# Gated DeltaNet's scan on one Trainium2 core: decayed keys, or a decay factor on the product's rows

## The chip, the cores and the metric

The kernel runs on one core of a Trainium2 chip. The metric is the device time of one execution in microseconds. The kernel is one layer of a hybrid sequence model with 512 latent tokens, 256 context tokens and 1024 channels, all in float32. Most large products split each operand into two parts, so that one product is three passes on TensorE; the small products inside the scans are plain float32.

The engines are TensorE (PE, and PEld for its weight loads), VectorE (DVE), ScalarE (ACT), GpSimd (POOL) and SyncE (SP), which issues all DMA transfers. Each engine works through its own queue in order.

## The reference, cut to what matters

The layer has three token mixers side by side (HGRN2, gated DeltaNet, S5), each projected and gated, then an output projection and a channel sub-layer. The change touches the gated DeltaNet alone. It has four heads with keys and values of 128 channels, runs in both directions, and the scan of the latent tokens starts from the final state of the context's. Per chunk the reference does this:

```python
def step(s, inp):
    qc, kc, vc, bc, gc = inp
    cum = jnp.cumsum(gc, axis=-1)                      # summed log decays in the chunk
    ...
    kb = kc * bc[..., None]
    m = jnp.where(strict, -jnp.einsum('bhtd,bhsd->bhts', kb, kc) * dmask, 0.0)
    rhs = jnp.concatenate([vc * bc[..., None], kb * jnp.exp(cum)[..., None]], axis=-1)
    sol = lax.linalg.triangular_solve(eye - m, rhs, left_side=True, lower=True, unit_diagonal=True)
    u, w = sol[..., :dv], sol[..., dv:]
    v_new = u - jnp.einsum('bhtd,bhdv->bhtv', w, s)
    ...
    s = (s * jnp.exp(last)[..., None]
         + jnp.einsum('bhsd,bhsv->bhdv', kc * jnp.exp(last - cum)[..., None], v_new))
```

The kernel solves with the inverse X of the unit triangular matrix: `v_new = X (b (v - exp(cum) (k S)))`, where `exp(cum)` is one number per token (a row of the product `k S`), b is beta over the key's squared norm, and v is rescaled to fit. The factor of a token may be put on the key before the product with S, or on the row of the product after it.

## The kernel before, in words

A chunk is 128 tokens: chunks 0 and 1 are the context's, 2 to 5 the latent's. Class `GD` handles a pair of heads; there are two pairs, so the scan runs twice. Both directions and both heads of the pair are worked on together, so an array of a step is 128 x (2 directions, 2 heads, 128), that is 128x512.

`run` first makes decays, keys in token layout and the inverses X of three batches of two chunks (`decays`, `tokens`, `batch`, `invert`), then goes through six steps, i = -2 to 3: two of the context, four of the latent. The state S is there from i = -1 on, so five steps of a pair use it. A step is:

- L930: product pk of the keys with the state S, four units (direction, head), on PE, into PSUM
- L932: r = v - pk, on VectorE
- L939: product py of X with r, on PE
- L944: u = py times b, on VectorE
- L950, L954, L956 (L958 where there is no state yet): the next state, S times the chunk's decay plus a product of ke and u

`ahead` (L903) prepares one step ahead what doesn't need the state. For the five steps with a state it loads the summed log decays of the step's chunks from the DRAM array `gdrow`, broadcast onto all 128 partitions (`rows`, L779; 128x512 float32, 256 KB), takes their Exp in place (L910) and multiplies with the transposed keys (L911); the result R is the first operand of L930. For all steps but the last it makes the decayed keys ke in token layout (L914).

`out` loads rows of the same kind, for two chunks at once (512 KB), for the queries: Exp at L1002, products with the queries at L1006 and the output's products at L1017 and L1018. It is called twice per pair.

Everything is traced in the order of the program, and the Tile framework's scheduler then orders each engine's queue by readiness in its own model of time, so an instruction can stand ahead of one that comes earlier in the program. The scans are woven together with pieces of other work by `weave`: while a scan runs, projections (three passes L246, L247, L248) keep PE at work. Their weights come through `Stream`: a load of 512 KB, a copy to the high part on ScalarE (L225) and a subtraction for the low part on VectorE (L226). All `dma` calls (L63) go to SyncE's queue. Arrays come from pools by tag: "s2" has 12 buffers of 128x512, "s4" 8 of 128x1024.

Of the kernel before, what the change touches and what calls it, by code (L numbers as in the profile page):

```python
# [18 lines left out]
# which pieces go to which engine: adaLN's tiles (vector engine), (latent or context, block) of the modulated tokens'  # L19
# low parts, groups of the scan's inputs (GpSimd) and of its outputs (vector engine); after which of adaLN's tiles a  # L20
# tile of tokens is loaded
# [7 lines left out]
# columns of w_in  # L29
# [3 lines left out]
def ap(t, off, dims):  # L33
    """An access pattern on a tile's (or slice's) partitions, with free dims [step, count]."""
    return bass.AP(tensor=t.tensor, offset=t.offset + off, ap=[list(t.ap[0])] + [list(d) for d in dims])


class K:
    """What the parts share: engines, pools, constants."""

    #: buffers of a tag
# [23 lines left out]
    @contextmanager  # L65
    def queued(self, *engines):
        """What the block gives these engines comes after what they were given before it."""
        with ExitStack() as st:
            traced = self.nc.cur_bb.bb.instructions
            for e in engines:  # L70
                st.enter_context(self.tc.issue_after(next(i for i in reversed(traced) if i.engine == e.engine)))
            yield


# ---------------------------------------------------------------- small arithmetic

class Names:
    """Names for the arrays of a tile [128, n, w]."""
# [14 lines left out]
def exp_precise(v, out, x, s):  # L93
    """exp(x) to float32's accuracy, 0 under its range: powers of two and a polynomial."""
# [15 lines left out]
def inv_two_pi():  # L110
    """1 / (2 pi) as four constants of 12 bits each."""
# [10 lines left out]
def sincos_precise(v, sn, cs, y, s):  # L122
    """sin and cos of y: its turns are reduced with exact products, then polynomials."""
# [41 lines left out]
    # quarter turns  # L165
# [3 lines left out]
    v.scalar_tensor_tensor(cq, w, 4.0, cq, op0=OP.is_equal, op1=OP.subtract)   # -cos  # L169
    v.tensor_scalar(sq, q, 1.0, None, op0=OP.is_equal)  # L170
    v.scalar_tensor_tensor(sq, q, -1.0, sq, op0=OP.is_equal, op1=OP.subtract)  # -sin
# [9 lines left out]
def rsqrt(v, out, x, t):  # L181
    """1 / sqrt(x), x > 0; three arrays of one shape."""
# [8 lines left out]
def cmul(v, outr, outi, ar, ai, br, bi, t):  # L191
    """Complex product; t is of the outputs' shape."""
# [8 lines left out]
# ---------------------------------------------------------------- products of split operands  # L201

class Stream:
    """Weights from DRAM, each split into two float32r parts that add up to it; a product of two
    split operands is three passes."""
# [13 lines left out]
    def split(self, w, engine=None):  # L219
        """Two parts of a tile of weights."""  # L220
# [8 lines left out]
    def load(self, w, col, nk, m=128, row=0):  # L229
        """The split block w[row:row + 128 nk, col:col + m], [128, nk, m]."""  # L230
# [4 lines left out]
def split_act(K, hi, lo, x, scale=None, engine=None):  # L235
    """hi + lo = scale * x."""
# [14 lines left out]
# ---------------------------------------------------------------- S5  # L251

class S5:
    """Chunks of 8 tokens. Partitions are (direction, state), or (token in chunk, channel of a group)."""
# [5 lines left out]
    def load(self, lam, b, c):  # L260
        """lam [128, 3 32]: its real and imaginary parts and the log of the step; b and c [128, 2 512]."""
# [10 lines left out]
    def params(self):  # L272
# [20 lines left out]
        # Bbar = ((a - 1) / lambda) B  # L293
# [21 lines left out]
        # powers by the token in the chunk: what it adds to the state after the chunk, times one  # L315
        # step more; and, the last token first, what that state gives at it
# [9 lines left out]
        # by blocks of 8 groups: [channel of a group, group, (token in chunk, chunk)], the context's chunks first  # L326
# [4 lines left out]
    def spread(self, e, x, p, g0, n, negate, o):  # L331
        """o [128, 2, n, (8 16)]: x [128, 2, G, 16] times p [128, 2, G, 8], complex; its imaginary part negated."""
# [55 lines left out]
    def taken(d, off, step, n):  # L388
        """An array [16, 8, ...] in DRAM as [(8 positions step apart, 16), 8, n]."""
        return bass.AP(tensor=d.tensor, offset=d.offset + off, ap=[[step, 8], [d.shape[-1], 128], [1, n]])  # L390

    def load_c(self, o):
        """C with its imaginary part negated, of both directions."""
# [6 lines left out]
    def spread_c(self, e, c, g0, n, o):  # L400
        """The parts of C's conjugate [128, 2, G, 16] times pout's: o [128, 2, n, (8 16)], its real part and its
        imaginary part's negative."""
# [9 lines left out]
    def taps(self):  # L412
        """The kernels of both directions over a chunk, in DRAM as [input channel, group, ...] with the lags in a row,
        the greatest first."""
# [5 lines left out]
        # Bbar of the two directions in columns 0..15 and 32..47  # L420
# [28 lines left out]
    def outputs(self):  # L449
        """-> self.dy: of the latent, as du, the last token of a chunk first."""  # L450
        K, G, n, m = self.K, self.G, 4, 8
        nc, v = K.nc, K.nc.vector
        # in the place of the context's states
# [44 lines left out]
# ---------------------------------------------------------------- HGRN2  # L498

class HG:  # L500
    """One head: q [128, 512] (twice the silu), F [128, 2 (bwd, fwd), 512], FC [128, 2, 256] of the
    context, V [128 tokens, 6 chunks, 128], the context's first. Chunks of 128; within one, both
    directions' decays to a common point between two blocks, for blocks of 1, 2, ... 64."""
# [35 lines left out]
    def levels(self):  # L539
        K, q, F, N = self.K, self.q, self.F, self.N  # L540
        nc, v = K.nc, K.nc.vector
        Q = self.Q = K.t("s4", [128, 2, N])       # q: suffix bwd, prefix fwd
        Y = self.Y = K.t("s4", [128, 2, N])       # k: suffix fwd, prefix bwd
# [28 lines left out]
        self.tot = tot                            # [128, (bwd, fwd), chunk]  # L572
# [23 lines left out]
    def out(self, norm_w, gate, dst):  # L596
        """Normed and gated, into dst [128 channels, 512] in DRAM. gate: twice its silu, [128, 512]."""
# [21 lines left out]
def norm_heads(K, out, po, nq):  # L619
    """RMSNorm over the last axis of po [128 tokens, 4, 128], which is twice the values, or has yet to  # L620
    be multiplied by nq [128, 4]; without the gain, and times 1/2, as the gate comes twice as large."""
# [17 lines left out]
# ---------------------------------------------------------------- gated DeltaNet  # L639

class GDScalars:
    """Per token: beta, the summed log decays, for all heads; columns (chunk, direction, head)."""

    def __init__(self, K, ba, a_log, dt_bias):
# [17 lines left out]
        # softplus(x) = max(x, 0) + 2 atanh(e / (2 + e)), e = exp(-|x|)  # L662
# [14 lines left out]
        # sums over the chunk up to each token, and from it  # L677
# [15 lines left out]
        # [(direction, pair of heads), chunk, (head, token)]  # L693
# [5 lines left out]
class GD:  # L699
    """Heads 2p and 2p + 1. Chunks of 128: 0, 1 are the context's, 2..5 the latent's. Keys, queries  # L700
    and values come as twice their silu. Directions 0 fwd, 1 bwd. A batch is two chunks, four units
    (chunk, head)."""

    def __init__(self, K, sc, p):
# [12 lines left out]
        self.sm = K.t("gsm", [128, 240], bufs=2)  # L717
# [15 lines left out]
    def two(x, y):  # L733
        """The arrays x and y of one tile, [128, ...] each, as [128, 2, ...]."""
# [3 lines left out]
    def tokens(self):  # L738
        """Keys into token layout, and the sums of squares of keys and queries; then what follows from them."""
# [27 lines left out]
        # beta / |k|^2, units (chunk, direction, head), and the same negated  # L767
# [4 lines left out]
        for d in range(2):  # L772
            v.tensor_tensor(self.bk[:, :, d], four(sc.beta)[:, :, d], n2, op=OP.mult)
        hv = hn.rearrange("p (c h) -> p c h", c=6)
# [186 lines left out]
    def run(self, norm_w, gate, dst):  # L961
# [6 lines left out]
        for d in range(2):  # L968
            K.nc.vector.tensor_copy(self.cum[:, :, d], cum[:, :, d])
# [676 lines left out]
```

## Time and profile before

| | |
|---|---|
| median of 3 runs | 1439.66 us (1438.58 to 1440.03) |
| span of the profiled execution | 1440.3 us |
| PE busy | 1283.4 us, 89% of the span |
| VectorE busy | 882.4 us, 61% |
| ScalarE busy | 505.7 us, 35% |
| GpSimd busy | 382.2 us, 27% |
| DMA | 163.94 MB, mean 114 GB/s |

The profiled execution is one run; its time is not listed apart from its span. Busy shares are means over stages with different limits, so the stretches in which PE stands still are read one by one. The scan of heads 0 and 1 lies at about 655 to 712 us, that of heads 2 and 3 at about 850 to 912 us. "PEclk" is the clock that TensorE was granted, as a share of full speed.

### The profile page before, as it was taken

How to read it: one execution, taken by the hardware profiler on the slowest of the kernel's cores; microseconds unless marked ns; L12 is line 12 of the kernel's file. 1: busy time of each engine (PE TensorE's matmuls, PEld its weight loads, DVE VectorE, ACT ScalarE, POOL GpSimd, SP SyncE). 2: the span in 40 equal slices, each digit the busy share in tenths (PEclk: the TensorE clock that was granted, in tenths of full speed). 3: DMA queues.
4: the chain of work that ended last, by engine and by line, in shares of the span. 5: the costliest groups of instructions: out<-in, count | busy, mean ns of one | idle time of the engine just before them, and what ended most of it. 6: DMA issues, size and time to landing. Idle time of an engine off the chain costs nothing. (4 is left out here: it accounts for less than half of the span.)

```text
span 1440.3 us, 18357 instructions
## 1 busy us (share of the span) xinstructions
PE 1283.4 (89%) x6829; PEld 1053.9 (73%) x6829; DVE 882.4 (61%) x1683; ACT 505.7 (35%) x887; POOL 382.2 (27%) x510
## 2 busy tenths in 40 slices
PE   7687999999899898898877979976999999999995
PEld 2376767888787786797655968854777888888884
DVE  7733387866669658895559756526777432544336
ACT  3427413432334455312244342313225422244222
POOL 0345699994006710000004550003104000000002
PEclk9899999999999899999989979989999999999998
DMA  7672342738647666824466684696406433333231
GB/s 296 110 153 45 47 62 40 112 51 65 105 72 118 75 159 136 100 31 84 115 107 222 211 173 91 149 193 221 139 27 184 127 94 96 91 100 103 91 100 60
DMA packets 184987, 163.94 MB, mean 114 GB/s; under 512 B 24960, under 2 KB 155200, under 8 KB 184896
## 3 DMA queue, kind: packets, MB, share of 16 engines
q1 hardware_dynamic: 184896, 162.76, 51.7%
q8 instruction: 54, 0.88, 0.3%
q14 instruction: 37, 0.30, 0.1%
HBM read 143.86 MB, written 18.87 MB: 113 GB/s over the span
## 5 line engine op out<-in xcount | busy, mean ns | idle before, releaser
L226 DVE TENSOR_TENSOR lo<-raw,hi 128x1024 fp32r<-128x1024 f32 (+1 forms) x161 | 190.5, 1184 | 264.3 <-ACT hi L225 264.0
L225 ACT ACTIVATE hi<-raw 128x1024 fp32r<-128x1024 f32 (+1 forms) x161 | 157.5, 979 | 392.0 <-PE pj L247 230.1
L246 PE MATMUL pj<-hh,hi 128*128 128x512 f32 (+1 forms) x520 | 216.9, 417 | 13.8 <-ACT hi L225 7.3
L247 PE MATMUL pj<-hl,hi 128*128 128x512 f32 (+1 forms) x520 | 214.8, 413 | 0.9 <-POOL hl L1153 0.8
L248 PE MATMUL pj<-hh,lo 128*128 128x512 f32 (+1 forms) x520 | 214.2, 412 | 0.9 <-DVE lo L226 0.9
L247 PE MATMUL pj<-hc,hi 128*128 128x512 f32 (+2 forms) x536 | 188.2, 351 | 1.7 <-DVE hc L239 0.8
L246 PE MATMUL pj<-h,hi 128*128 128x512 f32 (+1 forms) x304 | 117.1, 386 | 12.7 <-ACT hi L225 11.6
L246 PEld LDWEIGHTS pj<-hh,hi 128*128 128x128 f32 (+1 forms) x520 | 101.8, 196 | 33.8 <-ACT hi L225 8.3
L248 PE MATMUL pj<-h,lo 128*128 128x512 f32 (+1 forms) x304 | 116.8, 385 | 3.4 <-DVE lo L226 3.1
L247 PEld LDWEIGHTS pj<-hl,hi 128*128 128x128 f32 (+1 forms) x520 | 101.8, 196 | 21.3 <-POOL hl L1153 2.4
L248 PEld LDWEIGHTS pj<-hh,lo 128*128 128x128 f32 (+1 forms) x520 | 101.7, 196 | 21.2 <-DVE lo L226 1.6
L247 PEld LDWEIGHTS pj<-hc,hi 128*128 128x128 f32 (+1 forms) x536 | 102.3, 191 | 16.2 <-DVE hc L1153 1.2
L246 PE MATMUL pj<-hc,hi 128*128 128x256 f32 (+2 forms) x264 | 85.8, 325 | 17.9 <-ACT hc L238 10.1
L1589 POOL TENSOR_TENSOR xn<-x,row 128x512 f32<-128x512 f32 x8 | 10.4, 1303 | 313.0 <-DVE x L1493 307.0
L248 PE MATMUL pj<-hc,lo 128*128 128x256 f32 (+2 forms) x264 | 85.5, 324 | 2.9 <-DVE lo L226 2.9
L1296 POOL TENSOR_TENSOR s<-s,raw 128x1024 f32<-128x1024 f32 x21 | 53.4, 2548 | 121.1 <-ACT raw L1295 111.3
L246 PEld LDWEIGHTS pj<-h,hi 128*128 128x128 f32 x304 | 57.8, 191 | 26.9 <-ACT hi L225 15.4
L248 PEld LDWEIGHTS pj<-h,lo 128*128 128x128 f32 x304 | 58.0, 191 | 17.3 <-DVE lo L226 6.8
L246 PEld LDWEIGHTS pj<-hc,hi 128*128 128x128 f32 (+1 forms) x264 | 50.9, 193 | 21.8 <-ACT hc L238 10.3
L248 PEld LDWEIGHTS pj<-hc,lo 128*128 128x128 f32 (+1 forms) x264 | 50.9, 193 | 6.6 <-DVE lo L226 3.7
L239 POOL TENSOR_TENSOR act<-raw,act 128x1024 fp32r<-128x1024 f32 x8 | 19.2, 2396 | 133.3 <-PE pj L247 110.5
L383 POOL TENSOR_TENSOR sw<-sp,sv 128x64 f32<-128x64 f32 x94 | 52.1, 554 | 0.0
(533 smaller groups left out, 2771.5 us busy)
## 6 DMA issues: line engine op xcount, KB each, us to landing
raw<-in_w_in SPq DMA_DIRECT2D x72, 512.0 KB
raw<-in_w_ff SPq DMA_DIRECT2D x64, 512.0 KB
raw<-in_ada_w SPq DMA_DIRECT2D x40, 512.0 KB
s<-gdrow SPq DMA_DIRECT2D x18, 256.0 KB
dg<-fg SPq DMA_DIRECT2D x16, 256.0 KB
fg<-dg SPq DMA_DIRECT2D x16, 256.0 KB
mg<-fg SPq DMA_DIRECT2D x16, 256.0 KB
fg<-mg SPq DMA_DIRECT2D x16, 256.0 KB
```

The lines of the kernel that those rows point to most:

```text
L225: K.nc.scalar.activation(hi, w, AF.Copy)
L226: (engine or K.nc.vector).tensor_tensor(lo, w, hi.bitcast(FT), op=OP.subtract)
L239: (engine or K.nc.vector).tensor_tensor(lo, x, hi.bitcast(FT), op=OP.subtract)
L246: nc.tensor.matmul(out, wh, xh, start=start, stop=False)
L247: nc.tensor.matmul(out, wh, xl, start=False, stop=False)
L248: nc.tensor.matmul(out, wl, xh, start=False, stop=stop)
L383: e.tensor_tensor(t[:, 0], aa[:, 0], x, op=OP.mult)
L1296: nc.gpsimd.tensor_tensor(acc, acc, w, op=OP.add)
L1589: nc.gpsimd.tensor_tensor(t[:, s], x1[i][:, s], fw[:, s], op=OP.mult)
```

## The change

The five decayed-key arrays of a pair are no longer made. L930 takes the plain transposed keys, and the factor exp(cum) of a token is applied when the product leaves PSUM: four instructions with a factor per row (one for each direction and head) compute `pk * ec - v` in place of one subtraction `v - pk`. The result has the opposite sign, and L944 takes a negated b (`nbk`) in the steps that have a state. The factors `ec` (24 columns) are one Exp of the summed log decays per pair, `nbk` one negation per pair; the small array `gsm` grows from 240 to 244 columns. `rows` loses the form for a step; `out` and `decays` still use it. The rest of the diff takes out comments.

```diff
@@ GD.tokens
             v.tensor_tensor(self.bk[:, :, d], four(sc.beta)[:, :, d], n2, op=OP.mult)
+        v.tensor_scalar(at(220, 24), at(100, 24), -1.0, None, op0=OP.mult)
@@ GD.rows
-    def rows(self, tag, c, d=None):
+    def rows(self, tag, c):
-        R = K.t(tag, [128, 2, 4, 128] if d is None else [128, 2, 2, 128])
+        R = K.t(tag, [128, 2, 4, 128])
-        step = 256 * (c[1] - c[0])
-        if d is not None:
-            K.dma(R, at(0, [[3072 + step, 2], [1, 256]]))
-        elif step == 256:
+        if c[1] == c[0] + 1:
@@ GD.ahead
-    def ahead(self, i, ch, final):
+    def ahead(self, ch, final):
-        nc, v = K.nc, K.nc.vector
-        R = ke = None
-        if i > -2:
-            R = self.rows("s2", ch, 0)
-            nc.scalar.activation(R, R, AF.Exp)
-            v.tensor_tensor(R, R, self.two(self.kT(ch[0]), self.kT(ch[1])), op=OP.mult)
-        if not final:
-            ke = K.t("s2", [128, 2, 2, 128])
-            v.tensor_tensor(ke, self.two(self.kt(ch[0]), self.kt(ch[1])), self.wide(self.el, ch), op=OP.mult)
-        return R, ke
+        if final:
+            return None
+        ke = K.t("s2", [128, 2, 2, 128])
+        K.nc.vector.tensor_tensor(ke, self.two(self.kt(ch[0]), self.kt(ch[1])), self.wide(self.el, ch), op=OP.mult)
+        return ke
@@ GD.step
-                    nc.tensor.matmul(pk[:, d, h], R[:, d, h], S[:, d, h], start=True, stop=True)
+                    nc.tensor.matmul(pk[:, d, h], self.kT(ch[d])[:, h], S[:, d, h], start=True, stop=True)
             r = K.t("s2", [128, 2, 2, 128])
-            v.tensor_tensor(r, vt, pk, op=OP.subtract)
+            for d in range(2):
+                for h in range(2):
+                    v.scalar_tensor_tensor(r[:, d, h], pk[:, d, h], self.ec[:, ch[d], d, h:h + 1], vt[:, d, h],
+                                           op0=OP.mult, op1=OP.subtract)
-        v.tensor_tensor(u, py, self.wide(self.bk, ch), op=OP.mult)
+        v.tensor_tensor(u, py, self.wide(self.bk if S is None else self.nbk, ch), op=OP.mult)
@@ GD.run
-        self.cum, self.el, self.last = four(124), four(148), four(172)
+        self.cum, self.el, self.last, self.ec, self.nbk = (four(o) for o in (124, 148, 172, 196, 220))
+        K.nc.scalar.activation(self.sm[:, 196:220], self.sm[:, 124:148], AF.Exp)
-        nxt = self.ahead(-2, order[0], False)
+        nxt = self.ahead(order[0], False)
-            now, nxt = nxt, self.ahead(i + 1, order[i + 3], i == 2) if i < 3 else None
-            yield from self.step(i, order[i + 2], *now)
+            now, nxt = nxt, self.ahead(order[i + 3], i == 2) if i < 3 else None
+            yield from self.step(i, order[i + 2], now)
```

## Rows read from the trace of the kernel before

**Rows 1.** The page, part 1: busy us (share of the span) x instructions

```profile
PE 1283.4 (89%) x6829; PEld 1053.9 (73%) x6829; DVE 882.4 (61%) x1683; ACT 505.7 (35%) x887; POOL 382.2 (27%) x510
```

**Rows 2.** Busy time by stretch, heads 0 and 1; columns in the first line

```profile
core 0: us, PE busy (x) PEld busy (x) DVE busy (x) ACT busy (x) POOL busy (x), PEclk, DMA share, GB/s
...
659.90:665.70 5.80, 0.04 (x1) 0.00 (x0) 1.29 (x2) 1.26 (x2) 0.00 (x0) 0.75 0.20 46
665.70:670.20 4.50, 4.46 (x19) 4.08 (x20) 1.89 (x3) 0.00 (x0) 0.00 (x0) 0.57 0.20 48
...
686.40:692.90 6.50, 0.23 (x2) 0.02 (x1) 3.25 (x6) 3.63 (x5) 0.00 (x0) 0.78 0.12 42
692.90:697.10 4.20, 4.20 (x14) 3.72 (x15) 2.95 (x4) 0.00 (x0) 0.00 (x0) 0.52 0.22 62
```

**Rows 3.** Order of time, first hole: start, duration, engine, line, [idle <-releaser]

```profile
657.49 1.06 PE L939 MATMUL mm<-s,s 128*128 128x128 f32 x8
...
659.54 0.40 PE L247 MATMUL pj<-hl,hi 128*128 128x512 f32 x1
663.73 0.63 ACT L910 ACTIVATE s<-s 128x512 f32<-128x512 f32 x1 [9.69 <-DMA s<-gdrow]
664.39 0.69 DVE L911 TENSOR_TENSOR s<-s,s 128x512 f32<-128x512 f32 x1 [6.01 <-ACT s L910]
...
665.00 0.68 DVE L944 TENSOR_TENSOR s<-mm,gsm 128x512 f32<-128x512 f32 x1
...
665.74 2.08 PE L954 MATMUL mm<-s,s 128*128 128x128 f32 x8 [5.80 <-DVE s L944]
```

**Rows 4.** Order of time, second hole

```profile
688.57 0.63 ACT L910 ACTIVATE s<-s 128x512 f32<-128x512 f32 x1 [11.49 <-DMA s<-gdrow]
...
689.85 1.06 ACT L1002 ACTIVATE s<-s 128x1024 f32<-128x1024 f32 x1 [0.66 <-DMA s<-gdrow]
...
690.94 0.69 DVE L1006 TENSOR_TENSOR s<-s,hc 128x512 f32<-128x512 f32 x1 [0.42 <-ACT s L1002]
...
691.55 0.68 DVE L1185 SCALAR_TENSOR_TENSOR s<-pst,pj 128x512 f32<-128x512 f32 x1
692.15 0.68 DVE L932 TENSOR_TENSOR s<-hc,mm 128x512 f32<-128x512 f32 x1
...
692.88 2.08 PE L939 MATMUL mm<-s,s 128*128 128x128 f32 x8 [6.26 <-DVE s L932]
```

**Rows 5.** Third hole, heads 2 and 3: two stretches, VectorE and PE in order

```profile
863.90:866.90 3.00, 0.19 (x2) 0.06 (x1) 1.40 (x3) 2.06 (x3) 0.27 (x1) 1.00 0.62 122
866.90:871.00 4.10, 4.10 (x15) 3.49 (x16) 4.07 (x6) 0.63 (x1) 0.00 (x0) 0.58 0.36 116
...
865.50 0.69 DVE L911 TENSOR_TENSOR s<-s,sv 128x512 f32<-128x512 f32 x1 [3.16 <-ACT s L910]
...
866.85 1.44 PE L954 MATMUL mm<-s,s 128*128 128x128 f32 x8 [2.81 <-DVE s L944]
```

**Rows 6.** Durations: lines by ns min/median/max, and four of L849 in order

```profile
L910 ACT ACTIVATE s<-s x10: 616/629/632, 663.7 to 878.8; 128x512 f32<-128x512 f32 x10
...
L932 DVE TENSOR_TENSOR s<-sv,mm x5: 677/687/689, 861.0 to 906.0; 128x512 f32<-128x512 f32 x5
...
L592 DVE SCALAR_TENSOR_TENSOR hs<-hs,ht,mm x24: 336/346/349, 268.4 to 512.6; 128x128 f32<-128x128 f32 x24
...
571.51 1.10 DVE L849 TENSOR_SCALAR s<-upper,gu 128x128 f32<-128x128 f32 x4
```

**Rows 7.** SyncE's DMA issues in order of time, around the second hole

```profile
677.36 0.37 SPq L63 DMA_DIRECT2D raw<-in_w_in  x1
677.79 4.89 SPq L63 DMA_DIRECT2D s<-gdrow  x3
```

**Rows 8.** After the scans: ScalarE's longest wait (us, times, longest), one stretch

```profile
ACT h L238 <- DMA t<-nb: 21.4, 4, 14.0
...
940.00:950.00 10.00, 6.96 (x24) 5.05 (x23) 4.50 (x6) 3.33 (x5) 0.00 (x0) 0.83 0.96 174
```

More of the change, by code (lines that the diff above doesn't have):

```diff
@@ L716, in __init__ @@
         self.vtc, self.ktc = (b.rearrange("p (c h d) -> p c h d", c=2, h=2) for b in base[5:7])
-        self.sm = K.t("gsm", [128, 240], bufs=2)
+        self.sm = K.t("gsm", [128, 244], bufs=2)
         self.sk = self.sm[:, 0:12].rearrange("p (c h) -> p c h", c=6)
@@ L901, in wide, with step @@
         return self.two(x[:, ch[0], 0], x[:, ch[1], 1])[:, :, :, None].to_broadcast([128, 2, 2, 128])
-    def ahead(self, i, ch, final):
+    def ahead(self, ch, final):
         K = self.K
-        nc, v = K.nc, K.nc.vector
-        R = ke = None
-        if i > -2:
-            R = self.rows("s2", ch, 0)
-            nc.scalar.activation(R, R, AF.Exp)
-            v.tensor_tensor(R, R, self.two(self.kT(ch[0]), self.kT(ch[1])), op=OP.mult)
-        if not final:
-            ke = K.t("s2", [128, 2, 2, 128])
-            v.tensor_tensor(ke, self.two(self.kt(ch[0]), self.kt(ch[1])), self.wide(self.el, ch), op=OP.mult)
-        return R, ke
-    def step(self, i, ch, R, ke):
+        if final:
[3 more added lines that the diff above has]
+        return ke
+    def step(self, i, ch, ke):
         K = self.K
```

## The prediction

> **What bounds the kernel now.** The page comes first: TensorE (PE) is busy for 89% of the span and VectorE (DVE) for 61% [rows 1]. A kernel of this kind gains where PE stands still, so the next view is the busy time by stretch over the two scans that the change touches (heads 0 and 1 near 655 to 712 us, heads 2 and 3 near 850 to 912 us). Heads 0 and 1 have two holes: PE has 0.04 us of work in one stretch of 5.8 us and 0.23 us in one of 6.5 us, and after each it runs for 4.5 and 4.2 us with a granted clock of 0.57 and 0.52 [rows 2]. These are parts at about half speed (the 1.2 GHz level), so a hole costs more than its width.
>
> The third view is the order of time around each hole. In the first, PE's last products for the context step (L939) are over at 658.6 us. Their eviction (L944) needs nothing else, yet it starts at 665.00, because VectorE works in order and L911, the product of keys and decay, stands ahead of it. L911 waits for the Exp of L910, which waits 9.69 us for the broadcast load of the decay rows. PE's L954 waits for L944 all that time: 5.80 us idle [rows 3]. So a transfer for the *next* step holds up the *present* one.
>
> The second hole has the same head: L910 waits for its load until 688.57, then L911. But more stands there. L1002, the Exp of the rows for the output product, waited for a load of its own until 689.85; behind it on VectorE are L1006 and L1185, and only then L932, on which PE's L939 waits: 6.26 us [rows 4].
>
> The third, in the scan of heads 2 and 3, is a small one like the first: L911 at 865.50 behind its Exp, then L944, with 2.81 us of PE idle inside a 3.0 us stretch and 4.1 us at clock 0.58 behind it [rows 5]. Elsewhere in both scans PE is full: the projections woven in hide the steps.
>
> **The change part by part.** Gone in each pair of heads, for five steps: the 256 KB broadcast load of decay rows, its Exp (0.629 us) and the product with the keys, which has the form of L932 (128x512, 0.687 us) [rows 6]. The state product L930 keeps its shape; only its first operand is another array.
>
> *First hole.* Without L910 and L911, L944 follows L939 at once, near 658.6, and is over at 659.3. PE has woven-in work until 659.9, so L954 starts with no hole. Saved: 5.80 idle, and the slow part: 4.5 x (1 - 0.57) = 1.9 [rows 2, 3]. Sum 7.7 us. Next late is the eviction L958 behind L954, which already has products of a projection beside it.
>
> *Third hole.* The same, since L944 stood behind L911 alone: 2.81 + 4.1 x (1 - 0.58) = 1.7, sum 4.5 us [rows 5].
>
> *Second hole.* Whole, it is 6.26 + 4.2 x (1 - 0.52) = 2.0, that is 8.3 us [rows 2, 4]. It goes whole only if L932 no longer stands behind L1006. If VectorE's order stays, L1002 still waits for its 512 KB of rows. What was in flight was the weights' load of 512 KB, the 256 KB for step 2, these 512 KB and the 256 KB for step 3, all issued from 677.4 to 682.7 [rows 7], and landed by 689.85, some 12 us for 1536 KB. Without the two of 256 KB a third of the bytes is gone. The one issued ahead is worth 12 x 256/1536 = 2.0 us; the one behind overlaps only the end, taken at half, 1.0. The bounds are 0 and 4.0, I take 3.0, an estimate from these rows. Then L932's first quarter is also ready 0.34 us earlier than the whole was (below). The hole shrinks by 3.3 us to 2.9; the slow part behind it is then like that of the third hole, 1.7 instead of 2.0. Saved 3.6 with the order as it stands, 8.3 with L932 ahead. A planner builds the orders, and lighter queues on SyncE, ScalarE and VectorE move it somewhat; I take 5.0, nearer to the order that the trace shows.
>
> The loads behind others in one queue deserve a sentence of the Trainium skill. The page "DMA: Bandwidth & Descriptors", section "Queues, rings and completion order", says that descriptors on a ring are consumed in order; by that alone only the load issued ahead would delay L1002's, the hole would shrink by 2.3 and the sum would be 1.0 us smaller. No row here separates the two.
>
> *Added on VectorE.* One subtraction of 128x512 (0.687 us) becomes four multiply-subtracts of 128x128 from PSUM with a factor per row. The trace has that form: L592 takes 0.346 us. How closely four follow each other is seen at L849, four of 128x128 in 1.10 us, so the four end after about 0.346 + 3 x 0.25 = 1.1 us [rows 6]. VectorE's own work falls: ten steps at 1.1 - 2 x 0.69 give -2.7 us; it is not the bound there. On the path the last quarter of r is 0.42 us later and the first 0.34 earlier. PE's L939 takes its four units one after another and needs the last some 0.7 us after the first, and in the undisturbed steps its start is covered by projection products. So I take 0. The ends are ten steps at +0.42, +4.2 us, if PE meets the last quarter each time, and ten at -0.34, -3.4 us, if the first decides; both stay for the range.
>
> A rule of the Trainium skill speaks against this part: "VectorE: DVE Perf Modes", section "Rules for kernel authors", wants the number of VectorE instructions kept small, and its section on the errata gives each one a fixed cost. With the page's fitted (N + 151)/0.96 ns four of 128 cost 1.16 us and one of 512 0.69 us. The trace agrees within 0.1 us [rows 6], so by the page the sum would lose at most 4.7 us, if no step were hidden.
>
> *Small edits.* Two Exps of 24 columns (each at most L910's 0.629) and two negations (each at most L592's 0.346) come before the batches, off the scans: 0 taken, at most 2.0 us [rows 6]. The sign of r is undone in L944's factor: no instruction. Where a factor is read from a small array that VectorE or ScalarE wrote over a hundred microseconds earlier, nobody waits.
>
> *Queues and buffers.* Ten loads leave SyncE's queue. One issue there stood blocked for a buffer while the weights' load was queued behind it, but the weights' load waits for a buffer of its own in the same place, so no more is counted. Ten fewer buffers of the tag "s2" are used; keys are read until L930 of the last step, but queries in the same buffer are read later still by L1006, so nothing is held longer.
>
> *Does it reach the end?* All engines work in order, and loads are issued when PE's work frees buffers, so what a scan gains shifts what follows. The last branch begins with the scan's result read back from DRAM: ScalarE waits 21.4 us for it [rows 8]. There the transfers are 0.96 busy [rows 8], the one place where a shift may be lost in part; since these loads too are released by the stage before them, I take nothing off.
>
> Sum: 7.7 + 5.0 + 4.5 = 17.2 us. The profiled execution spans 1440.3 us; its time is not listed apart from the three runs (1438.58 to 1440.03 us), and the span is 0.6 us above their median. 1440.3 - 17.2 - 0.6 = 1422.5 us.
>
> **The rivals.** (a) *All three holes go.* The planner puts L932 ahead of L1006. For it: L1006 has no hurry. Against it: it stood ahead in the trace. 7.7 + 8.3 + 4.5 = 20.5, 1419 us, and to 1416 with the early first quarter.
>
> (b) *The wait for the output's rows takes the place of the one removed.* L1002 stays where it is, its load lands no sooner, and the quarters cost their +4.2 on the path. For it: that load was as late as L910's, 1.3 us apart [rows 4]. Against it: a third of the bytes is gone. 7.7 + 4.5 - 4.2 = 8.0, 1431.7 us.
>
> (c) *Slower.* With ten issues and ten Exps gone, the planner, which holds transfers to be quicker than the trace shows, places the Exps of the output rows (two in each pair, L1002) earlier, before their data are there. ScalarE's queue then stands at them, and behind it L225, the splitting of the weights, on which PE's projections wait, as well as VectorE's L1006 ahead of L932 and L944. Each such Exp that is waited for costs a hole like the first or second, about 8 us. From three new holes on (24 against 20.5 saved) the kernel is slower: with four, 1439.7 - 20.5 + 32 = 1451 us; with three and the quarters' 4.2, 1447. Against it: these loads need buffers that are free only when batches are done.
>
> (d) *It doesn't do what it says for the time.* The releaser is inferred; if PE at the three places really waited for weights, the holes stay and nothing but the quarters changes: 1438 to 1441 us. Against it: L944's own input was there 6.4 us before it started [rows 3].
>
> **How the numbers follow.** Forecast as above 0.45, its own range 1417 to 1428; (a) 0.20; (b) 0.20; (c) 0.08; (d) 0.07. The range is 1414 to 1437 us: from (a) with the quarters' gain and a little of order elsewhere, to (b) with a few us lost in the stage of the transfers; it leaves out (c), (d) and a little at the lower end. A difference of 0.2% (2.9 us) is about what a measurement of this kernel can tell from no change. Faster by more 0.84, within it 0.08, slower 0.08.
>
> **What would show it.** Right: no L910 or L911 lines; L944 starts less than 1 us after L939 in the context steps; no PE hole over 1 us in the first and third place, granted clock 1.00 through them; a hole of 0 to 3 us before L939 of the second latent step, ended by L932 behind L1006; four lines of about 0.35 us at the subtraction; the stages behind 720 us shifted whole. Wrong: PE waiting for L944 or L939 as long as before, with L1002 waiting over 3 us for its load, or new waits of L225 behind it.

## The result and the profile after

The changed kernel takes 1419.51 us (median of 4 runs, 1418.70 to 1422.16). The kernel before takes 1439.53 us beside it, the ratio is 0.9872 with a 95% interval of 0.9855 to 0.9888. That is 20.0 us less; 17.2 were forecast, and 1422.5 us lies 3.0 us above the result.

In after's profile every line of the scan stands 3 to 8 lines higher: L930 is now L922, L932 is L927 (four instructions), L939 is L935, L944 is L940, L954 is L950; L1002 and L1006 of `out` are L999 and L1003. The page's part 1 of after, busy us (share of the span) x instructions, against [rows 1]:

```profile
PE 1277.2 (90%) x6829; PEld 1048.5 (74%) x6829; DVE 879.2 (62%) x1705; ACT 501.2 (35%) x879; POOL 381.5 (27%) x510
```

PE has the same 6829 products and VectorE 22 instructions more. What changed is when PE works. Busy time by stretch in after, at the places of [rows 2] and [rows 5] (stretch, length, busy us of PE, PEld, DVE, ACT, POOL, granted clock, DMA share, GB/s):

```profile
640.00:660.00 20.00, 20.00 (x154) 18.79 (x153) 16.40 (x25) 6.12 (x10) 0.00 (x0) 1.00 0.47 72
660.00:680.00 20.00, 20.00 (x119) 16.63 (x117) 14.72 (x27) 4.04 (x5) 1.69 (x2) 1.00 0.25 48
680.00:700.00 20.00, 20.00 (x131) 17.17 (x129) 11.04 (x35) 3.52 (x11) 0.00 (x0) 1.00 0.34 53
...
840.00:860.00 20.00, 20.00 (x116) 17.18 (x116) 15.13 (x29) 4.89 (x6) 1.75 (x2) 0.96 0.41 85
860.00:880.00 20.00, 20.00 (x125) 17.41 (x124) 11.24 (x31) 3.32 (x11) 0.00 (x0) 1.00 0.59 91
```

The third number is PE's busy time: 20.00 of 20 us in all five stretches. The same view of before, second and third stretch:

```profile
660.00:680.00 20.00, 14.26 (x78) 12.41 (x79) 10.85 (x17) 3.32 (x5) 1.70 (x2) 0.83 0.17 34
680.00:700.00 20.00, 13.73 (x72) 11.43 (x71) 8.87 (x13) 3.63 (x5) 0.00 (x0) 0.83 0.36 85
```

All three holes are gone, the second too, and with them the slow parts. (The 0.96 comes from the first two microseconds of its stretch, at 0.59; they follow short waits of PE near 831 and 835 us, 0.9 us for L890 and 0.8 for L225, neither at the place of a hole. From 842 us on the clock is 1.00.)

The order of time in after around the places of the first and the second hole (start, duration, engine, line, [idle before it <-releaser]; SPq rows are DMA issues; in a long row, which joins several, a later one stood blocked):

```profile
653.57 0.37 SPq L63 DMA_DIRECT2D raw<-in_w_in  x1
653.99 0.78 SPq L63 DMA_DIRECT2D s<-gdrow  x1
673.76 0.37 SPq L63 DMA_DIRECT2D raw<-in_w_in  x1
...
658.61 1.06 PE L935 MATMUL mm<-s,s 128*128 128x128 f32 x8
...
659.71 0.69 DVE L940 TENSOR_TENSOR s<-mm,gsm 128x512 f32<-128x512 f32 x1 [0.21 <-PE mm L935]
...
660.45 1.16 PE L950 MATMUL mm<-s,s 128*128 128x128 f32 x8
...
671.01 1.05 ACT L999 ACTIVATE s<-s 128x1024 f32<-128x1024 f32 x1
...
674.94 1.29 DVE L1003 TENSOR_TENSOR s<-s,hc 128x512 f32<-128x512 f32 x2
...
679.75 1.12 DVE L927 SCALAR_TENSOR_TENSOR s<-mm,gsm,hc 128x128 f32<-128x128 f32 x4
```

First place: the eviction L940 now waits only 0.21 us for its own product, where L944 had stood for 6 us behind L911 [rows 3], and L950 follows without idle time. Second place: on VectorE the order is still the one forecast, L1003 stands ahead of L927. But L999 waits for nothing. The load of its rows was issued at 653.99, 17 us before, and ahead of the next weights' load, which got its buffer only at 673.76. In the kernel before it was issued at 678.41, behind a weights' load and a load of decay rows, the first of the three in the row [rows 7].

Where the rest of the time went is read from the waits of PE over both scans, 640 to 920 us (line waited for: us in total, times, longest), here of before, without the lines of [rows 3] to [rows 5], which come to 14.9 us:

```profile
PE pj L246 <- ACT hc L238: 10.1, 1, 10.1
PE mm L892 <- DVE s L893: 8.7, 2, 7.8
...
PE tr L854 <- DVE s L851: 4.5, 2, 2.4
PE pj L248 <- DVE lo L226: 2.9, 1, 2.9
```

and of after:

```profile
PE tr L851 <- DVE s L848: 6.7, 2, 5.5
PE mm L889 <- DVE s L890: 6.7, 3, 5.0
PE pj L246 <- ACT hc L238: 4.8, 1, 4.8
PE pj L248 <- DVE lo L226: 4.1, 1, 4.1
PE tr L1024 <- DVE s L636: 3.0, 1, 3.0
...
```

All waits of this view add up to 44.7 us before and 27.6 after. The scans' waits are gone, the projections' wait for ScalarE's L238 is half as long, the waits at the transposes have grown (L851, which is L854 in before, from 4.5 to 6.7 us, L1024 from 0.2 to 3.0), and one of 1.3 us before L1014 is new. By stage, from the starts of the same instructions in both traces:

| from (line in before) | to | before, us | after, us | difference |
|---|---|---|---|---|
| start | first py of heads 0, 1 (L939) | 657.5 | 658.6 | +1.1 |
| | first transposes of the output (L1027) | 56.0 | 41.4 | -14.6 |
| | first gated add after the scans (L1493) | 316.9 | 307.3 | -9.6 |
| | end of the span | 409.9 | 409.3 | -0.6 |
| sum | | 1440.3 | 1416.6 | -23.7 |

The second row holds holes one and two. The third holds the third hole and everything else from the end of the first scan to the first gated add. The spans differ by 23.7 us and the medians by 20.0: the two profiled executions are single runs. That of after took 1418.70 us at a span of 1416.6 us, 2.1 us above it. In every run of the kernel before that has both figures the time lies 1.7 to 1.8 us above the span, so its profiled execution took some 1442.1 us, an estimate.

### The profile page after: what moved, and what is told of

It reads as the page before. It is cut to its first block, busy times and chain, and to the rows that moved or that the text cites. A ratio compares the mean times of both kernels' runs of the same rounds, so it can differ in the third digit from the quotient of the medians.

```text
span 1416.6 us, 18347 instructions
## 1 busy us (share of the span) xinstructions
PE 1277.2 (90%) x6829; PEld 1048.5 (74%) x6829; DVE 879.2 (62%) x1705; ACT 501.2 (35%) x879; POOL 381.5 (27%) x510
## 5 line engine op out<-in xcount | busy, mean ns | idle before, releaser
L226 DVE TENSOR_TENSOR lo<-raw,hi 128x1024 fp32r<-128x1024 f32 (+1 forms) x161 | 190.0, 1180 | 266.4 <-ACT hi L225 266.2
L225 ACT ACTIVATE hi<-raw 128x1024 fp32r<-128x1024 f32 (+1 forms) x161 | 157.6, 979 | 396.8 <-PE pj L247 222.8
L246 PE MATMUL pj<-hh,hi 128*128 128x512 f32 (+1 forms) x520 | 215.4, 414 | 15.6 <-ACT hi L225 8.7
```

Source lines behind the costliest of these rows:

```text
L225: K.nc.scalar.activation(hi, w, AF.Copy)
L226: (engine or K.nc.vector).tensor_tensor(lo, w, hi.bitcast(FT), op=OP.subtract)
L246: nc.tensor.matmul(out, wh, xh, start=start, stop=False)
```

## The experiments

Every kernel ran beside the kernel before on the same chip (its medians were 1438.7 to 1439.9 us). In the profiles of these kernels the line numbers are shifted again; the text names the line of before or after.

### What of the removed work cost the time: the chain or the loads

**The chain put back as dead work.** The changed kernel gets the load, the Exp and the product back; nobody reads the result.

```diff
-    def ahead(self, ch, final):
+    def ahead(self, ch, final, dead=True):
...
+        if dead:
+            R = K.t("s2", [128, 2, 2, 128])
+            src = self.sc.drow
+            K.dma(R, bass.AP(tensor=src.tensor, offset=src.offset + 1536 * self.p_ + 256 * ch[0],
+                             ap=[[0, 128], [3072 + 256 * (ch[1] - ch[0]), 2], [1, 256]]))
+            K.nc.scalar.activation(R, R, AF.Exp)
+            K.nc.vector.tensor_tensor(R, R, self.two(self.kT(ch[0]), self.kT(ch[1])), op=OP.mult)
```

> The changed kernel, with the load, the Exp and the product of the decayed keys put back as dead work whose result nobody reads. Theory 'queues' (no data dependence is needed, only an instruction that waits for a transfer in front of L940 in VectorE's order): the three holes come back, 1436 to 1443 us. Theory 'data' (the state product had to wait for its own operand): the holes stay away, since the plain keys are there, and the dead work is hidden: 1419 to 1424 us.

Measured: 1437.76 us (10 runs), ratio 0.9986 (0.9975 to 0.9997). Waits of PE from 640 to 720 us, and the order of time at the first hole (its L942 and L957 are before's L939 and L954, its L947 is L944):

```profile
PE mm L942 <- DVE s L934: 6.3, 1, 6.3
PE mm L957 <- DVE s L947: 5.7, 1, 5.7
```

```profile
663.54 0.63 ACT L908 ACTIVATE s<-s 128x512 f32<-128x512 f32 x1 [9.63 <-DMA s<-gdrow]
...
664.20 0.69 DVE L909 TENSOR_TENSOR s<-s,s 128x512 f32<-128x512 f32 x1 [5.95 <-ACT s L908]
664.81 0.68 DVE L947 TENSOR_TENSOR s<-mm,gsm 128x512 f32<-128x512 f32 x1
...
665.55 2.08 PE L957 MATMUL mm<-s,s 128*128 128x128 f32 x8 [5.74 <-DVE s L947]
```

Both holes of the first scan are back with their old widths (6.26 and 5.80 us before), although no product depends on the restored array. In the second scan 1.2 us come back, before L939 and not before L954. So what stopped PE is not the data but the place: L909 stands in VectorE's queue ahead of the eviction and waits.

**The loads alone put back.** The same without the Exp and the product: ten dead loads of 256 KB.

```diff
...
+            K.dma(R, bass.AP(tensor=src.tensor, offset=src.offset + 1536 * self.p_ + 256 * ch[0],
+                             ap=[[0, 128], [3072 + 256 * (ch[1] - ch[0]), 2], [1, 256]]))
```

> The changed kernel with the ten broadcast loads alone put back; nobody reads them. They take their buffers of the tag s2, SyncE's queue and the transfers' bandwidth. Theory 'queues': VectorE and ScalarE wait for none of them, so holes one and three stay away; the output's rows stand behind four of them in SyncE's queue and come later, so the second hole may be back in part: 1420 to 1428 us. Theory 'traffic' (the bytes and the blocked issues cost the time by themselves): 1434 us or more.

Measured: 1422.26 us (4 runs), ratio 0.9882 (0.9867 to 0.9897), inside the changed kernel's interval. Of the three holes one of 1.1 us is left (at L939 of before). That is 17.6 us below the kernel before beside it, against 20.0 and, in a second measurement below, 17.4 for the change: a price of the 2.6 MB and the ten issues can't be told from nothing. The Exp and the product that wait for them make the difference to the run above.

**The chain kept in the kernel before, its load taken away.** The Exp reads the keys, which are long there, instead of loaded rows. Exp, product and the single subtraction stay; the decay is left out.

```diff
-            R = self.rows("s2", ch, 0)
-            nc.scalar.activation(R, R, AF.Exp)
+            R = K.t("s2", [128, 2, 2, 128])
+            nc.scalar.activation(R, self.two(self.kT(ch[0]), self.kT(ch[1])), AF.Exp, scale=1e-6)
```

> The kernel before, but the array of decayed keys is made without its broadcast load: Exp of the keys times 1e-6 (so about 1) instead of the Exp of the loaded rows; Exp, product and the single subtraction stay. The decay is left out of the state product by that. Theory 'loads' (the time came from the late transfers in front of the eviction): the holes before L954 in the context steps of both scans go, 7.7 + 4.5 us; in SyncE's queue the output's rows now stand directly behind a weights' load that waits for its buffer, so the second hole, before L939 of the second latent step, stays in part (2 to 6 us): 1420 to 1428 us. Theory 'work' (the time came from ten Exps and ten products less on ScalarE and VectorE): nothing but the wait is gone, the work is there, 1435 to 1440 us.

Measured: 1433.36 us (10 runs), ratio 0.9958 (0.994 to 0.9976): between what the two theories gave, so neither bound held. Its profiled run is the slowest of the ten (1440.48 us), so it serves for where the waits are, not for the sum. Waits of PE, 640 to 720 us:

```profile
PE mm L1017 <- DVE s L1006: 6.3, 1, 6.3
PE mm L939 <- DVE s L932: 3.7, 1, 3.7
```

and the order of time of SyncE's issues, ScalarE and VectorE in the same kernel:

```profile
650.87 17.59 SPq L63 DMA_DIRECT2D raw<-in_w_in  x2
668.51 0.57 SPq L63 DMA_DIRECT2D s<-gdrow  x1
...
677.09 1.06 ACT L1002 ACTIVATE s<-s 128x1024 f32<-128x1024 f32 x1 [9.36 <-DMA s<-gdrow]
...
678.18 1.29 DVE L1006 TENSOR_TENSOR s<-s,hc 128x512 f32<-128x512 f32 x2 [4.87 <-ACT s L1002]
679.39 0.68 DVE L932 TENSOR_TENSOR s<-hc,mm 128x512 f32<-128x512 f32 x1
```

The first hole is gone (there is no wait for L944, nor is there one in the second scan), as it should be if the load was its cause. The second is the forecast's own picture: with the decay rows away, L1002 still waits for the output's rows, and L932 stands behind L1006, 3.7 us. A third wait, 6.3 us before the output's product, is new. The rows stand behind a weights' load that stood blocked on SyncE for some 17 us: the row of 17.59 joins two issues, and the second came 17.2 us after the first.

### The second hole: who set its end

**The output's first rows loaded ahead of the scan, in the kernel before.**

```diff
+        R34 = self.rows("s4", (3, 4))
         nxt = self.ahead(-2, order[0], False)
...
-                yield from self.out((3, 4), norm_w, gate, y)
+                yield from self.out((3, 4), norm_w, gate, y, R34)
```

> The kernel before, with the load of the output's first rows (512 KB, L1002's) issued ahead of the scan instead of in its middle. It tells what the second hole waited for. If for the output's rows: the hole of 6.26 us before L939 shrinks to under 3 us, 1433 to 1437 us. If for the decayed keys' own load (L910, L911): the hole keeps 4 us or more, 1436 to 1441 us. Holes one and three stay.

Measured: 1441.25 us (10 runs), ratio 1.0013 (1.0 to 1.0026): no gain, perhaps a small loss. The hole follows the first theory; the time is just above the range of the second. Waits of PE from 640 to 720 us:

```profile
PE mm L954 <- DVE s L944: 5.6, 1, 5.6
PE mm L939 <- DVE s L932: 2.7, 1, 2.7
```

The second hole falls from 6.26 to 2.7 us and not to zero: now L911, behind the load of its own decay rows, holds L932. So two loads held the second hole, 1.3 us apart in the trace of before [rows 4], and taking either away leaves a hole: 2.7 us here, 3.7 us in the kernel without L910's load. The time didn't follow the narrower hole; waits for L226 and L225 further on grew instead (2.9 to 9.4 and 0.3 to 4.1 us).

**Two wide instructions in place of the four quarters, in the changed kernel.**

```diff
-            for d in range(2):
-                for h in range(2):
-                    v.scalar_tensor_tensor(r[:, d, h], pk[:, d, h], self.ec[:, ch[d], d, h:h + 1], vt[:, d, h],
-                                           op0=OP.mult, op1=OP.subtract)
+            v.tensor_tensor(r, pk, self.wide(self.ec, ch), op=OP.mult)
+            v.tensor_tensor(r, r, vt, op=OP.subtract)
```

> The changed kernel, with two instructions of 128x512 (product times the broadcast factors, then minus v) in place of the four of 128x128. VectorE's work in a step is 1.3 us instead of 1.1, and r is ready at once at its end, not in quarters. Theory 'covered': no difference that can be measured to the changed kernel, 1417 to 1423 us. Theory 'chain' (each step waits for r): ten times 0.2 to 0.9 us, 1421.5 to 1429 us.

Measured: 1434.37 us (12 runs), ratio 0.9974 (0.9962 to 0.9987): a miss, most of the gain is lost. The order of time on SyncE, ScalarE and VectorE shows by what (its L997 and L1001 are L999 and L1003 of after), and the waits of PE from 640 to 720 us:

```profile
652.84 17.66 SPq L63 DMA_DIRECT2D raw<-in_w_in  x2
670.55 0.57 SPq L63 DMA_DIRECT2D s<-gdrow  x1
...
679.11 1.06 ACT L997 ACTIVATE s<-s 128x1024 f32<-128x1024 f32 x1 [9.79 <-DMA s<-gdrow]
...
680.20 1.29 DVE L1001 TENSOR_TENSOR s<-s,hc 128x512 f32<-128x512 f32 x2 [3.51 <-ACT s L997]
```

```profile
PE mm L933 <- DVE s L926: 3.6, 1, 3.6
```

The first hole stays away, but the planner (the Tile framework's scheduler) has put the output's rows *behind* the weights' load, which stands blocked for its buffer, where the changed kernel has them ahead of it. The rows are there at 679.1 and the second hole is there again, 3.6 us, with a clock of 0.83 in the stretch 680 to 700; the second scan has one of 2.7 us of the same kind.

**The same, with the output's first rows loaded ahead of the scan.** The edit is that of the rows above, on top of the two wide instructions.

> The kernel with two wide instructions (e7_two_wide), and the load of the output's first rows issued ahead of each scan. Theory 'place of the rows' (e7's 15 us over the changed kernel come from that load standing behind a weights' load that waits for its buffer): the holes of 3.6 and 2.7 us go, 1419 to 1426 us. Theory 'chain' (the two wide instructions themselves make each step longer): 1431 us or more.

Measured: 1424.98 us (5 runs), ratio 0.9905 (0.9887 to 0.9924). Busy time by stretch, same columns as above:

```profile
660.00:680.00 20.00, 20.00 (x116) 16.54 (x115) 14.67 (x21) 3.09 (x4) 1.70 (x2) 1.00 0.20 41
680.00:700.00 20.00, 20.00 (x130) 17.20 (x131) 10.49 (x24) 4.35 (x12) 0.00 (x0) 1.00 0.28 40
```

Both holes are gone, that of the second scan too. The kernel is now 13.8 us below the kernel before on its chip, where the last one was 4.8: 9.0 us come back, so the place of the rows' load, not the two wide instructions themselves, had cost most. To the changed kernel (17.4 us below on the same chip, 20.0 in its first runs) 4 to 6 us remain; no single wait in the trace stands for them, and they stay open. The planner ordered other work differently too: between the first py and the output's transposes PE is as full here as in the changed kernel, but for 44.6 us against 41.4, with 272 products there against 259.

**The rows loaded ahead of the scan in the changed kernel itself.** The same edit on the changed kernel.

> The changed kernel, with the load of the output's first rows issued ahead of each scan by hand. In the changed kernel that load already came in time: the second scan's ScalarE waited 6.3 us for it, with PE busy. Theory 'in time is enough': within 3 us of the changed kernel, 1417 to 1422 us. If the wait in the second scan costs something that its PE record hides: 1416 us or less.

Measured: 1421.44 us (6 runs), ratio 0.9878 (0.9855 to 0.99), the same as the changed kernel. Landing in time is enough.

**The rows' load held back in the changed kernel.** A one-column copy on GpSimd writes into the rows' buffer and reads the first latent step's u, so the load can't be issued sooner.

```diff
         R = K.t(tag, [128, 2, 4, 128])
+        if after is not None:
+            K.nc.gpsimd.tensor_copy(R[:, 0, 0, 0:1], after)
...
-        R = self.rows("s4", c)
+        R = self.rows("s4", c, self.w[0][:, 0, 0, 0:1] if c == (3, 4) else None)
```

> The changed kernel, with the load of the output's first rows held back by a one-column copy that needs u of the first latent step (near 672 us in the first scan, where it was issued at 654). Theory 'place of the rows': a hole of 2 to 6 us before L940 or L935 of the first scan comes back, with a slow stretch behind it, and a smaller one may come in the second: 1424 to 1432 us. If the rows had no part in the second hole: 1418 to 1422 us.

Measured: 1416.54 us (4 runs, 1413.45 to 1425.14), ratio 0.9855 (0.9827 to 0.9883): a miss, there is no loss. Order of time on SyncE, ScalarE and VectorE (its L1001 and L1005 are L999 and L1003), and the wait of PE:

```profile
650.70 0.37 SPq L63 DMA_DIRECT2D raw<-in_w_in  x1
669.37 0.37 SPq L63 DMA_DIRECT2D s<-gdrow  x1
671.07 0.37 SPq L63 DMA_DIRECT2D raw<-in_w_in  x1
...
673.22 1.06 ACT L1001 ACTIVATE s<-s 128x1024 f32<-128x1024 f32 x1 [4.99 <-DMA s<-gdrow]
674.32 1.29 DVE L1005 TENSOR_TENSOR s<-s,hc 128x512 f32<-128x512 f32 x2 [1.68 <-ACT s L1001]
```

```profile
PE mm L937 <- DVE s L929: 0.3, 1, 0.3
```

The load is issued at 669.37, only 1.2 us sooner than in the kernel with two wide instructions, and yet L1001 starts 3.85 us after the issue, there 679.11 - 670.55 = 8.56 us. The difference that the rows show is what stands ahead: here the weights' load comes 1.7 us behind it, there it had just been issued before. So a late issue alone did no harm here; one behind 512 KB of weights did.

The Trainium skill's page "DMA: Bandwidth & Descriptors", section "Queues, rings and completion order", says that descriptors are consumed in ring order; the three traces agree (3.85 us with the weights behind, 8.56 and 8.58 us with them ahead).

### The quarters alone

In the kernel before the subtraction becomes four multiply-subtracts with a factor of one, and b is negated as in the change. Loads, Exp and product stay.

```diff
-            v.tensor_tensor(r, vt, pk, op=OP.subtract)
+            for d in range(2):
+                for h in range(2):
+                    v.scalar_tensor_tensor(r[:, d, h], pk[:, d, h], self.one[:, 0:1], vt[:, d, h],
+                                           op0=OP.mult, op1=OP.subtract)
```

> The kernel before, with its loads, Exps and products, but the subtraction from PSUM made as four multiply-subtracts of 128x128 with a factor of 1, and the negated b in the eviction. It is the price of the quarters alone. Theory 'covered' (woven-in products hide the later quarters): 1438 to 1442 us, the three holes as before. Theory 'on the path' (each of ten steps pays 0.42 us, or each VectorE instruction its fixed cost): 1442.5 us or more. Theory 'first quarter' (L939 starts 0.34 us earlier in each step): 1437 us or less.

Measured: 1437.16 us (12 runs), ratio 0.9988 (0.9976 to 1.0). Waits of PE from 640 to 720 us:

```profile
PE mm L943 <- DVE s L935: 6.4, 1, 6.4
PE mm L958 <- DVE s L948: 5.8, 1, 5.8
```

The two holes stand as they did. The time lies between the ranges of "first quarter" and "covered", at most 3.5 us less than before and not more. Four instructions of 0.34 us, the last of them done some 0.4 us later than the single one, cost nothing here: PE doesn't wait for the last. In the first such step of after (rows not shown) the four start at 663.59, and PE's first weight load for L935 starts at 664.00. The page "VectorE: DVE Perf Modes" of the Trainium skill, section "Rules for kernel authors", asks for few instructions; the prediction's estimate from that page's fitted time was up to 4.7 us more, and this run excludes it.

### Each pair alone

The change in heads 0 and 1 alone, with the old form in heads 2 and 3:

```diff
...
+            if R is not None:
+                v.tensor_tensor(r, vt, pk, op=OP.subtract)
-            for d in range(2):
+            for d in range(2 if R is None else 0):
```

> The change in heads 0 and 1 alone; heads 2 and 3 as before. Theory 'holes': the first and second hole go, the third stays: a shift of 13 to 16 us at the end of the first scan that is kept to the end, 1423 to 1427 us. If what is gained in the first scan is lost again before the second (transfers that are late anyway): 1430 us or more.

Measured: 1423.51 us (4 runs), ratio 0.99 (0.9882 to 0.9917), 15.6 us less. And in heads 2 and 3 alone:

> The change in heads 2 and 3 alone; heads 0 and 1 as before. Theory 'holes': the third hole alone goes, 4.5 us, and up to 2.5 us behind it: 1432 to 1436 us, with the first two holes as before. If the two parts help each other only together: within 2 us of the kernel before.

Measured: 1436.40 us (10 runs), ratio 0.9981 (0.9965 to 0.9998), 2.7 us less and just above the range expected, with holes of 6.7 and 5.8 us left in the first scan. The parts add up to 18.3 of the 20.0 us. In the kernel that keeps the old form in heads 2 and 3 there is no wait before L954 in the second scan and one of 0.9 us before the next step's L939, so its 15.6 us hold a part of the third hole. There the decay rows of the step came in time: L944 follows L911 at 847.28 and PE goes on without a gap.

### The changed kernel once more

> The changed kernel itself once more beside the other three, so that differences of a few us among them are read on one chip: 1417 to 1423 us, with a run-to-run spread of some 4 us as its neighbours show.

Measured: 1421.30 us (4 runs, 1418.79 to 1421.57), ratio 0.9875 (0.9858 to 0.9891). The 1416.54 us with the rows held back lie below it, but that kernel's runs reach from 1413 to 1425 us, so no version that beats the changed kernel is shown.

## Why the prediction was right, and where its steps were off

**First hole: right.** 7.7 us were booked. VectorE waits 0.21 us for the eviction's own product, and PE goes on without a gap. The dead chain brings the hole back at 5.7 us, the dead loads don't; that settles the cause as the prediction gave it: an instruction that waits for a load, ahead of an eviction in an in-order queue.

**Second hole: the term was too small.** The step that failed is "L1002 still waits for its 512 KB of rows", and with it "no more is counted" under the queues: VectorE's order stayed as forecast, but in SyncE's queue the rows' load moved ahead of the blocked weights' load, from 678.41 to 653.99. 5.0 was booked, a hole of 2.9 us was to stay, and PE shows none. The first scan's stage lost 14.6 us, against 7.7 + 5.0 = 12.7 as booked and 7.7 + 8.3 = 16.0 with both holes whole. The rest is work, as the stage in before and in after shows:

```profile
657.50:713.50 56.00, 43.89 (x253) 37.13 (x252) 28.05 (x53) 9.76 (x20) 1.70 (x2) 0.88 0.36 75
658.60:700.00 41.40, 41.40 (x259) 35.11 (x257) 26.88 (x63) 7.56 (x16) 1.69 (x2) 1.00 0.31 56
```

12.1 us of idle PE and the 3.9 us of its slow parts are gone, and six products more lie in the stage, which is busy for 41.4 us at full clock against 43.9 - 3.9 = 40.0. The working behind the smaller term was near for the case that didn't come: the forecast's hole of 2.9 us is 3.7 us in the kernel without L910's load and 3.6 us with two wide instructions, where the rows do stand behind the weights. It took bytes in flight as the price; in these traces it counted which load was ahead in SyncE's queue.

**Rival (a)** gave the time to half a microsecond (1419), but not by its mechanism: L927 did not move ahead of L1003. That it met the time is luck in part. Why the planner put the load ahead of the weights' load in one kernel and behind it in another that differs by two VectorE instructions a step stays open; the runs show only that it does, and that setting it right is worth 9.0 us there.

**Third hole: gone as forecast, its size not settled.** 4.5 were booked; the change in heads 2 and 3 alone gives 2.7 (0.3 to 5.0 by its interval). A wait of PE behind an Exp that waits for its decay rows stands in the second scan of before (2.8 us), with the quarters alone (2.3), with the dead chain (1.2) and where heads 2 and 3 keep the old form (0.9), and in none of the traces of the changed kernel. So its width moves with the time at which the load comes.

**Quarters and small edits at nothing: right**, by the quarters alone (at most 3.5 us gained). **Rival (b)** falls with it and with the rows' early landing. **Rival (c)**, a planner that puts an Exp before its data are there, has the right place and the wrong price: with two wide instructions such waits came up, and 13 to 15 us of the gain were lost, 9.0 of them by the place of the rows' load, yet the kernel was not slower than before. **Rival (d)** is excluded by the trace of after.

**The shift to the end: right.** Nothing was lost behind the scans (-0.6 us in the last stage). The -9.6 us of the stage between, against the 4.5 booked, are not the change's alone. From the same mark to the same mark it is 316.9 us in before, but 309.6 with the dead chain and 312.3 with the quarters alone, where both holes of the first scan stand; a second trace of the changed kernel has 309.0. The wait for L238 is as short there (4.7 and 4.0 us) as in after (4.8), so its shortening is not what the missing holes bought. What the change gives in this stage beyond the third hole stays open.

**From span to time: the holes were read in a long run.** The prediction in effect took 17.2 us off the median, and its 0.6 us is the step from the span to that. But a time lies above its span, and before's profiled run, at some 1442.1 us, was 2.5 us slower than the median beside after's; after's own was 0.8 faster than its median. With 0.4 by which the two lie unequally above their spans this is 3.7, the difference between 23.7 and 20.0.

## What to carry to other kernels

Where an engine works in order, look not at what an eviction needs but at what stands ahead of it: work prepared for the next step that waits for a transfer stops the present one, and here an operation of more instructions without such a wait was cheaper. The place of a load in the issue queue, ahead of or behind one that is blocked for its buffer, was worth 9.0 us here, where the whole change gave 20.0; read it in both kernels before crediting an edit. A hole with two loads behind it closes only when nobody waits for either, so test the removal of each and of both.

## What the runs showed that was not expected

A broadcast load of 512 KB was used 3.85 us after its issue when no other load was ahead, and 8.56 and 8.58 us after it when a 512 KB load of weights had been issued just before. The bytes alone don't give the time: in before the 256 KB of the first hole, issued at 652.87 right behind a weights' load, were used only at 663.73, 10.9 us after. A single weights' load that waits for its buffer held SyncE's queue for some 17 us, with everything behind it.

Two kernels that differ in two VectorE instructions a step against four, at nearly the same busy time, are 13 to 15 us apart, for the most part by the order of two DMA issues: 9.0 us come back when the rows' load alone is moved ahead.
